# Stick-breaking attention: the second sigmoid and the running product moved from PSUM to SBUF, and the PSUM banks dealt out anew

## The chip, the cores and the metric

The kernel runs on one core of a Trainium2 chip. A core has a matrix engine (PE, with its weight loader PEld), a vector engine (DVE), an activation engine (ACT), a general engine (POOL) and DMA queues issued by SP. Each engine runs its own instructions in their written order and waits on semaphores for the others. Operands live in SBUF; matmuls write to PSUM, which has eight banks of 128 partitions by 512 fp32. POOL does not touch PSUM in this kernel. The metric is device time in microseconds, the median of several executions.

## What is computed

One decoder block in fp32 over 2048 tokens of width 1024: an input projection, eight attention heads beside a pooling branch, an output projection, then a gated feed-forward layer. The change touches the attention alone:

```python
for i in range(S // Q_BLOCK):                      # 128 queries at a time
    L = (i + 1) * Q_BLOCK
    z = jnp.einsum('bhqd,bhkd->bhqk', qb, kb) * inv_sqrt
    mask = s_idx < t_idx
    log1m = jnp.where(mask, -jax.nn.softplus(z), 0.0)
    after = lax.cumsum(log1m, axis=3, reverse=True) - log1m
    logw = jax.nn.log_sigmoid(z) + after
    w = jnp.where(mask, jnp.exp(jnp.where(mask, logw, 0.0)), 0.0)
    outs.append(jnp.einsum('bhqk,bhkd->bhqd', w, vb))
```

The kernel writes this without logarithms: the weight of key s is sigmoid(z_s) times the product of sigmoid(-z_j) over the later keys j up to the query. That product is a scan from right to left along a row.

## The kernel before

Matmuls run in single-pass fp32 with each operand split into a high and a low part (`split`, L57 to L60: ACT writes the high part, DVE or POOL subtracts to get the low one), so one product is two or three matmuls (`mm3`, L65 to L71).

**The attention stage** goes through 80 units (head h, query block tb, key block sc), with sc from tb down to 0, and 4 steps in each unit, one for each 128 queries: 320 steps. A unit with sc == tb is *diagonal*: its step i needs only (i+1)*128 keys, and a mask is added by one more matmul. All others are *full*, 128 queries by 512 keys in each step. In step n the program emits, in this order:

1. `weights_step` (L792): two matmuls make z in a PSUM bank (L801, L802), ACT takes sigmoid(z/8) to `sg` in SBUF (L806), and sigmoid(-z/8) in place in the z bank (L807).
2. `scan_step` (L810) of step n-1: POOL sets the column past the row's end, to 1 in a diagonal unit (L815) or to the product carried over from the key block to the right (L817); DVE scans the z bank from right to left into `pr` in SBUF (L818), starting from that same carry, which it reads out of the earlier `pr`; POOL multiplies `sg` by the shifted `pr` into `w` (L821). The scan's second tensor operand is not used (its operation is a bypass); `sg` is given for it.
3. `values_step` (L839), three turns behind: two matmuls add to `av`, the sum for (h, tb), over four to sixteen turns (L848, L849). After the last, ACT copies `av` to `o1` in SBUF (L853) and two DMAs store it.
4. `turn_step` (L825), seven steps behind the weights: PE transposes the `w` tiles into a PSUM bank (L833), ACT writes the high part `wth` (L59), DVE the low part `wtl` (L60).
5. Now and then a filler piece: three matmuls of the input projection for tokens still to come, in a bank of its own, with the work that goes with it.

No planner reorders this: every engine gets its instructions in the order in which the program emits them. The banks are dealt in turn: three for z, two for turned weights (`wt`), two for `av`, one for fillers (`mm`). A bank comes free when the last reader of what stood in it is done, and the next matmul into it waits for that. In SBUF there are five `sg` tiles, six `pr`, eleven `w` (OFF + 4), and four each of `wth` and `wtl`.

Of the kernel before, what the change touches and what calls it, by code (L numbers as in the profile page):

```python
# [9 lines left out]
F32 = mybir.dt.float32  # L10
F32R = mybir.dt.float32r
AF = mybir.ActivationFunctionType
ALU = mybir.AluOpType
# [4 lines left out]
P = 128  # L18
# [10 lines left out]
TB = 512  # L29
# [3 lines left out]
NEG = -1e30  # L33
LAG = 2
OFF = 7
ZB, WB = 3, 2
FT = {"sr": 4, "p1": 1, "u2": 2, "u3": 2, "u4": 1, "cu": 2, "s": 6, "gs": 3, "tr": 4, "gf": 1}
PAIRS, HELD = 6, 4
RB = PAIRS - 1
# [5 lines left out]
def block_kernel(ctx, tc, x, c, w_cond, b_cond, g_mix_pre, g_mix_post, w_in, w_pool,  # L45
                 pool_scale, w_out, g_ffn_pre, g_ffn_post, w_gate, w_up, w_down, out):
    nc = tc.nc
# [17 lines left out]
    def mm3(ps, terms, first=True, last=True):  # L65

        n = len(terms)
        for i, ((lh, ll), (rh, rl)) in enumerate(terms):
            nc.tensor.matmul(ps, lh, rh, start=first and i == 0, stop=False)  # L69
            nc.tensor.matmul(ps, lh, rl, start=False, stop=False)  # L70
            nc.tensor.matmul(ps, ll, rh, start=False, stop=last and i == n - 1)  # L71

    def open_pool(stack, name, bufs=1, side=None):
        kw = {"side": side} if side else {}
        return stack.enter_context(tc.tile_pool(name=name, bufs=bufs, reuse_waits="tile", **kw))
# [68 lines left out]
    def psum(tag, bufs, name):  # L144
        return psp.tile([P, TB], F32, tag=tag, bufs=bufs, name=name)

    turn = [0]

    def mm_ps(name, alone=False):
        turn[0] += 1  # L150
        return z_ps(name) if turn[0] % 2 and not alone else psum("mm", 1, name)

    z_ps = lambda name: psum("z", ZB, name)
    t_ps = lambda name: psum("wt", WB, name)
    av_ps = lambda name: psum("av", 2, name)

    ident_r = c1.tile([P, P], F32R, tag="ident_r", name="ident_r")
    nc.vector.tensor_copy(ident_r, ident)
# [2 lines left out]
    one = ones[:, 0:1]  # L161
# [149 lines left out]
    def tokens(tb, k, cols=slice(0, TB)):  # L311
        if tb == 1:
            both = ht[1][k // HK]
            return both[:, 0, k % HK, cols], both[:, 1, k % HK, cols]
        return ht[tb][0][:, k, cols], ht[tb][1][:, k, cols]
# [145 lines left out]
    def take_chunk(chunk, tb, ps):  # L461
        kind, m = chunk
        if kind == "u":
            ops = pool_ops(tb, ps, m)
            urgent.append(next(ops))
            small.append(ops)
        else:
            urgent.append(lambda: store_qk(tb, ps, (qd if kind == "q" else kd)[m], f"{kind}{m}"))
# [132 lines left out]
        modulate(1, kc, pt)  # L601

    first_ps = {}
    first_banks = {(0, 0): ("mm", 1), (0, 1): ("av", 2), (1, 1): ("av", 2)}

    def first_products(n, tb, *ks):
        if (n, tb) not in first_ps:
            first_ps[n, tb] = psum(*first_banks.get((n, tb), ("z", ZB)), f"first{n}_{tb}")
        ps = first_ps[n, tb]
        for k in ks:  # L610
            mm3(ps, [((loaded[n][1][:, k, :], loaded[n][2][:, k, :]), tokens(tb, k))], first=k == 0, last=k == KC - 1)
        if ks[-1] == KC - 1:
            take_chunk(chunks[n], tb, ps)
# [156 lines left out]
    att = open_pool(ph1, "att", bufs=2)  # L770
# [14 lines left out]
        nc.sync.dma_start(raw(vt), vd[tb][:, h, :].rearrange("(b p) e -> p b e", p=P))  # L785
        return qt

    qts, prevs, avs, wss = {}, {}, {}, {}

    scans = []  # L790

    def weights_step(u, i):  # L792

        h, tb, sc = u
        diag = sc == tb
        kt, qt = kv[h, sc][0], qts[h, tb]
        L = (i + 1) * P if diag else TB
        nm = f"{h}_{tb}_{sc}_{i}"
        z = z_ps(f"z{nm}")
        keys = kt[:, 0:L]  # L800
        nc.tensor.matmul(z[:, 0:L], qt[:, 0, i * P:(i + 1) * P], keys, start=True, stop=False)  # L801
        nc.tensor.matmul(z[:, 0:L], qt[:, 1, i * P:(i + 1) * P], keys, start=False, stop=not diag)  # L802
        if diag:
            nc.tensor.matmul(z[:, i * P:L], ident_r, neg_r, start=False, stop=True)  # L804
        sg = att.tile([P, TB], F32, tag="sg", bufs=5, name=f"sg{nm}")
        nc.scalar.activation(sg[:, 0:L], z[:, 0:L], AF.Sigmoid, scale=0.125)  # L806
        nc.scalar.activation(z[:, 0:L], z[:, 0:L], AF.Sigmoid, scale=-0.125)  # L807
        scans.append((u, i, z, sg, L, nm))

    def scan_step(u, i, z, sg, L, nm):  # L810

        diag = u[1] == u[2]
        pr = att.tile([P, TB + 1], F32, tag="pr", bufs=6, name=f"pr{nm}")
        if diag:
            nc.gpsimd.memset(pr[:, L:L + 1], 1.0)  # L815
        else:
            nc.gpsimd.tensor_copy(pr[:, L:L + 1], prevs[i][:, 0:1])  # L817
        nc.vector.tensor_tensor_scan(pr[:, 0:L][:, ::-1], z[:, 0:L][:, ::-1], sg[:, 0:L],  # L818
                                     one if diag else prevs[i][:, 0:1], ALU.mult, ALU.bypass)
        w = att.tile([P, TB], F32, tag="w", bufs=OFF + 4, name=f"w{nm}")  # L820
        nc.gpsimd.tensor_tensor(w[:, 0:L], sg[:, 0:L], pr[:, 1:L + 1], ALU.mult)  # L821
        prevs[i] = pr
        wss.setdefault(u, []).append(w)

    def turn_step(u, b):  # L825

        h, tb, sc = u
        i0 = b if sc == tb else 0
        lo0 = i0 * P
        nm = f"{h}_{tb}_{sc}_{b}"  # L830
        wt = t_ps(f"wt{nm}")
        for i in range(i0, 4):
            nc.tensor.transpose(wt[:, i * P:(i + 1) * P], wss[u][i][:, b * P:(b + 1) * P], ident)  # L833
        wh = att.tile([P, TB], F32R, tag="wth", bufs=4, name=f"wth{nm}")
        wl = att.tile([P, TB], F32R, tag="wtl", bufs=4, name=f"wtl{nm}")
        split(wh[:, lo0:], wl[:, lo0:], wt[:, lo0:])
        return wh, wl, lo0

    def values_step(u, b, wh, wl, lo0):  # L839
        h, tb, sc = u  # L840
        hp, j = h // 2, h % 2
        first = sc == tb and b == 0
        last = sc == 0 and b == 3
        if first:
            avs[h, tb] = av_ps(f"av{h}_{tb}")
        av = avs[h, tb]
        vb = kv[h, sc][1][:, b, :]
        nc.tensor.matmul(av[:, lo0:], vb, wh[:, lo0:], start=first, stop=False)  # L848
        nc.tensor.matmul(av[:, lo0:], vb, wl[:, lo0:], start=False, stop=last)  # L849
        if last:  # L850
            end = (h, tb) == (HEADS - 1, NTB - 1)
            o1 = (up if end else wsp).tile([P, TB], F32, tag="um" if end else "o1", bufs=1, name=f"o1_{h}_{tb}")
            nc.scalar.copy(o1, av)  # L853
            for part, dst in enumerate((mtd, mld)):
                (nc.scalar if end else nc.sync).dma_start(dst[tb][hp, j * DH:(j + 1) * DH, :], o1[part * DH:(part + 1) * DH])

    def unit_loads(u):
        h, tb, sc = u
        if sc == tb:
            qts[h, tb] = block_loads(h, tb)  # L860
# [23 lines left out]
        next(fill)  # L884
    taken = START
    attending = True
    steps = [(u, i) for u in units for i in range(4)]

    def wo_load():
# [5 lines left out]

    SEQUENCE = [sb * NT // 2 + half * 4 + i for sb in range(2) for i in range(4) for half in range(2)]
    mixed = {}
    banks = itertools.cycle([("z", ZB)] * ZB + [("mm", 1)] + [("wt", WB)] * WB + [("av", 2)] * 2)
    f_ps = lambda name: psum(*next(banks), name)

    def mix_load(T):
        tb, cols = T // 4, slice((T % 4) * P, (T % 4 + 1) * P)
# [48 lines left out]
    waiting = []  # L951
    spent = 0.0
    for n in range(len(steps) + OFF):
        if n < len(steps):
            u, i = steps[n]
            if i == 0:
                unit_loads(u)
            weights_step(u, i)
            spent += 2.5 if u[1] == u[2] else 4.0
        if len(scans) > 1 or n >= len(steps) and scans:  # L960
            scan_step(*scans.pop(0))
        if len(waiting) > LAG:
            values_step(*waiting.pop(0))
        if n >= OFF:
            u, b = steps[n - OFF]
            waiting.append((u, b, *turn_step(u, b)))
        goal = START + (N_PIECES - START) * spent / (4 * sum(area[:END]))
        while fill is not None and taken < goal:
            taken += 1
            if next(fill, 0) == 0:  # L970
                fill = None
        for pool, here in ((hb, not wo and taken >= HB_FREE), (ha, len(wo) == 4 and fill is None)):
            if here:
                hi, lo = (pool.tile([P, 4, D], F32R, tag=tag, name=f"wo_{pool.name}{tag}")
                          for tag in ("hi", "lo"))
# [596 lines left out]
```

## Time and profile before

| | |
|---|---|
| median of 3 runs | 2353.89 us (2349.65 to 2355.68) |
| the profiled execution | 2351.43 us |
| its span, first to last instruction | 2349.6 us |
| mean granted PE clock | 0.991 of full speed |
| attention stage | from 323.5 us (first z) to about 864 us |

The page gives each engine's busy time, then the span in 40 slices of 58.7 us with the busy share of each in tenths, then the groups of instructions. In a group's row stand line, engine, operation, result and operands with their shapes, the count, the busy time and the mean duration in ns of one, and behind the second bar the idle time of the engine just before these instructions and what ended it. A wait for several semaphores is put down to the one that came last by the profile; where the engine named had long been done, it was another. Matmuls are pipelined, so their recorded durations overlap. In a timeline row stand start and duration in us, and in brackets the idle time before it.

### The profile page before, as it was taken

What the parts mean: (1) busy time and instruction counts of PE and PEld (TensorE: products, weight loads), DVE (VectorE), ACT (ScalarE), POOL (GpSimd) and SP (SyncE); (2) the same over time, 40 slices, a digit from 0 to 9 for tenths busy, and PEclk for the clock granted to TensorE, in tenths of its full rate; (3) what the DMA queues carried; (4) which work ended last, traced back from release to release, by engine and by line L of the source; (5) the groups of instructions that cost most, each with busy time, mean ns of one, the idle gap of its engine ahead of it and who ended that gap; (6) DMA issues with size and microseconds to landing.
All of it is one profiled execution on the core that took longest, in us unless ns stands there. A gap on an engine that the chain in (4) does not pass through costs nothing.

```text
span 2349.6 us, 33532 instructions
## 1 busy us (share of the span) xinstructions
PE 2278.4 (97%) x10717; PEld 1866.6 (79%) x10717; DVE 1638.0 (70%) x2221; ACT 1179.3 (50%) x2411; POOL 1293.3 (55%) x1429
## 2 busy tenths in 40 slices
PE   6999999999999989999999999999999999999997
PEld 3778878888888768887888888788888888888885
DVE  6764549999999975757565565886776565555556
ACT  4323659899998864444222232454533323234444
POOL 4542337787677764544777778430475665641004
PEclk9999999999999999999999999999999999999998
DMA  8785764333443636656554555776763333327554
GB/s 287 244 293 193 273 189 117 90 105 90 126 113 95 190 99 196 220 193 203 163 167 153 162 161 179 264 243 201 257 196 101 119 110 95 114 86 279 193 196 144
DMA packets 307116, 405.18 MB, mean 172 GB/s; under 512 B 19254, under 2 KB 179578, under 8 KB 303868
## 3 DMA queue, kind: packets, MB, share of 16 engines
q1 hardware_dynamic: 302620, 400.68, 52.8%
q10 hardware_dynamic: 4320, 2.36, 0.4%
q8 instruction: 85, 1.39, 0.2%
q14 instruction: 91, 0.75, 0.1%
HBM read 274.51 MB, written 128.45 MB: 171 GB/s over the span
## 4 chain that ended last, share of the span: by engine, by line
PE 79%; DVE 7%; issue 4%; ACT 4%; POOL 3%; DMA 3%; SPq 0%; DVEq 0%; POOLq 0%; ACTq 0%
PE t_u L70 3%; PE t_u L69 3%; PE t_u L71 3%; PE t_g L70 3%; PE t_g L69 3%; PE t_g L71 3%; PE wt L833 3%; PE dn0p L70 3%; PE dn0p L71 3%; PE dn0p L69 3%; PE dn1p L70 3%; PE dn1p L69 3%; PE dn1p L71 3%; DVE pr L818 3%; PE b_g L70 2%
## 5 line engine op out<-in xcount | busy, mean ns | idle before, releaser
L821 POOL TENSOR_TENSOR w<-sg,pr 128x512 f32<-128x512 f32 (+2 forms) x320 | 306.1, 956 | 143.6 <-DVE pr L818 81.3
L1179 POOL TENSOR_TENSOR s<-s,cu 128x512 f32<-128x512 f32 x88 | 132.7, 1515 | 240.7 <-DVE cu L1178 140.1
L818 DVE TENSOR_TENSOR_SCAN pr<-z,pr,sg 128x512 f32<-128x512 f32 x192 | 244.5, 1274 | 0.5 <-POOL pr L817 0.5
L60 DVE TENSOR_TENSOR wtl<-wt,wth 128x512 fp32r<-128x512 f32 (+1 forms) x320 | 190.3, 595 | 35.0 <-ACT wth L59 33.0
L806 ACT ACTIVATE sg<-z 128x512 f32<-128x512 f32 (+2 forms) x320 | 175.0, 547 | 48.0 <-PE z L804 22.2
L59 ACT CAST wth<-wt 128x512 fp32r<-128x512 f32 (+1 forms) x320 | 173.1, 541 | 21.5 <-PE wt L833 19.8
L833 PE MATMUL wt<-ident,w 128*128 128x128 f32 x1088 | 172.0, 273 | 2.5 <-DVE wtl L60 2.2
L807 ACT ACTIVATE z<-z 128x512 f32<-128x512 f32 (+2 forms) x320 | 174.1, 544 | 0.0
L60 DVE TENSOR_TENSOR u_s_l<-u_s,u_s_h 128x512 fp32r<-128x512 f32 x66 | 66.4, 1007 | 151.9 <-ACT u_s_h L59 151.9
L833 PEld LDWEIGHTS wt<-ident,w 128*128 128x128 f32 x1088 | 133.5, 140 | 32.6 <-DVE wtl L60 3.7
L1169 ACT ACTIVATE s<-s 128x512 f32<-128x512 f32 x88 | 55.7, 633 | 192.6 <-DVE s L1168 192.6
L801 PE MATMUL z<-kt,qt 128*128 128x512 f32 (+2 forms) x320 | 128.8, 403 | 16.8 <-DVE pr L818 12.2
L70 PE MATMUL dn0p<-w0p_l,g0p_h 128*128 128x512 f32 x308 | 121.2, 394 | 1.9 <-DVE w0p_l L60 1.9
L848 PE MATMUL av<-wth,vt 128*128 128x512 f32 (+1 forms) x320 | 121.5, 380 | 0.0
L60 DVE TENSOR_TENSOR u_a_l<-u,u_a_h 128x512 fp32r<-128x512 f32 x66 | 77.4, 1175 | 62.3 <-ACT u_a_h L59 62.3
L69 PE MATMUL dn0p<-w0p_h,g0p_h 128*128 128x512 f32 x308 | 120.5, 391 | 0.0
L71 PE MATMUL dn0p<-w0p_h,g0p_l 128*128 128x512 f32 x308 | 120.4, 391 | 0.0
L59 ACT CAST g_s_h<-g_s 128x512 fp32r<-128x512 f32 x66 | 39.5, 620 | 157.6 <-POOL g_s L1111 81.5
L849 PE MATMUL av<-wtl,vt 128*128 128x512 f32 (+1 forms) x320 | 116.9, 365 | 0.0
L802 PE MATMUL z<-kt,qt 128*128 128x512 f32 (+2 forms) x320 | 116.7, 365 | 0.0
L59 ACT CAST u_s_h<-u_s 128x512 fp32r<-128x512 f32 x66 | 38.6, 614 | 152.2 <-POOL u_s L1111 152.2
L70 PE MATMUL dn1p<-w1p_l,g1p_h 128*128 128x512 f32 x292 | 114.4, 392 | 0.0
(655 smaller groups left out, 7266.2 us busy)
## 6 DMA issues: line engine op xcount, KB each, us to landing
g<-in_w_gate_dram SPq DMA_DIRECT2D x42, 512.0 KB, 4.6
u<-in_w_up_dram SPq DMA_DIRECT2D x42, 512.0 KB, 5.0
wc<-in_w_cond_dram SPq DMA_DIRECT2D x32, 512.0 KB, 5.8
qt<-qd SPq DMA_DIRECT2D x64, 256.0 KB, 3.9
wd<-in_w_down_dram SPq DMA_DIRECT2D x44, 256.0 KB, 3.0
tdt<-wd SPq DMA_DIRECT2D x44, 256.0 KB, 2.0
w0p<-tdt SPq DMA_DIRECT2D x44, 256.0 KB, 2.9
w1p<-tdt SPq DMA_DIRECT2D x44, 256.0 KB, 2.8
```

Of the source, the lines that this page charges most:

```text
L59: nc.scalar.copy(hi, src)
L60: low.tensor_tensor(lo, src, raw(hi), ALU.subtract)
L69: nc.tensor.matmul(ps, lh, rh, start=first and i == 0, stop=False)
L70: nc.tensor.matmul(ps, lh, rl, start=False, stop=False)
L71: nc.tensor.matmul(ps, ll, rh, start=False, stop=last and i == n - 1)
L801: nc.tensor.matmul(z[:, 0:L], qt[:, 0, i * P:(i + 1) * P], keys, start=True, stop=False)
L806: nc.scalar.activation(sg[:, 0:L], z[:, 0:L], AF.Sigmoid, scale=0.125)
L807: nc.scalar.activation(z[:, 0:L], z[:, 0:L], AF.Sigmoid, scale=-0.125)
L818: nc.vector.tensor_tensor_scan(pr[:, 0:L][:, ::-1], z[:, 0:L][:, ::-1], sg[:, 0:L], one if diag else prevs[i][:, 0:1], ALU.mult, ALU.bypass)
L821: nc.gpsimd.tensor_tensor(w[:, 0:L], sg[:, 0:L], pr[:, 1:L + 1], ALU.mult)
L833: nc.tensor.transpose(wt[:, i * P:(i + 1) * P], wss[u][i][:, b * P:(b + 1) * P], ident)
L1179: nc.gpsimd.tensor_tensor(s, s, u, ALU.mult)
```

## The change

The second sigmoid goes from the z bank to the `pr` tile in SBUF, so `pr` is now taken in `weights_step`; the scan runs in place in `pr`. For its unused operand it gets `idle`, a PSUM bank filled with zeros once. The carry is copied by POOL to a small tile of its own (`carry`, one column) after each scan that has a key block to its left: 192 of the 320. `values_step` moves from behind the scan to the head of the step. The banks are dealt anew during the attention: two for z, one for `idle`, three for turned weights, one for `av`, one for fillers. `bank_cycle` hands out single banks in turn; before and after the attention it gives the same turns as before.

```diff
-        nc.scalar.activation(z[:, 0:L], z[:, 0:L], AF.Sigmoid, scale=-0.125)
-        scans.append((u, i, z, sg, L, nm))
+        pr = att.tile([P, TB + 1], F32, tag="pr", bufs=PRB, name=f"pr{nm}")
+        nc.scalar.activation(pr[:, 0:L], z[:, 0:L], AF.Sigmoid, scale=-0.125)
+        scans.append((u, i, pr, sg, L, nm))
...
-        pr = att.tile([P, TB + 1], F32, tag="pr", bufs=6, name=f"pr{nm}")
-        if diag:
+        carry = carries.pop(i, None)
+        if carry is None:
             nc.gpsimd.memset(pr[:, L:L + 1], 1.0)
         else:
-            nc.gpsimd.tensor_copy(pr[:, L:L + 1], prevs[i][:, 0:1])
-        nc.vector.tensor_tensor_scan(pr[:, 0:L][:, ::-1], z[:, 0:L][:, ::-1], sg[:, 0:L],
-                                     one if diag else prevs[i][:, 0:1], ALU.mult, ALU.bypass)
+            nc.gpsimd.tensor_copy(pr[:, L:L + 1], carry)
+        nc.vector.tensor_tensor_scan(pr[:, 0:L][:, ::-1], pr[:, 0:L][:, ::-1], idle[:, 0:L],
+                                     one if carry is None else carry, ALU.mult, ALU.bypass)
+        if u[2]:
+            carries[i] = att.tile([P, 1], F32, tag=f"carry{i}", bufs=2, name=f"carry{nm}")
+            nc.gpsimd.tensor_copy(carries[i], pr[:, 0:1])
...
+    idle = psum("z2", 1, "idle")
+    nc.vector.memset(idle, 0.0)
+    z_ps, t_ps, av_ps, mm_only = bank_cycle(*('z0', 'z1')), bank_cycle(*('w0', 'w1', 'a1')), bank_cycle(*('a0',)), bank_cycle(*('mm',))
...
     for n in range(len(steps) + OFF):
+        if len(waiting) > LAG:
+            values_step(*waiting.pop(0))
         if n < len(steps):
...
             scan_step(*scans.pop(0))
-        if len(waiting) > LAG:
-            values_step(*waiting.pop(0))
```

What this does to the order on PE is seen at the unit (head 4, query block 2, key block 0). In a name such as `z4_2_0_1` stand head, query block, key block and step; the last number is the buffer's. PE before, from one z to the next, with the engines whose semaphores a row waits for:

```order
L801 MATMUL z4_2_0_0_7300<-kt4_0_6774,qt4_2_7096 128x512 [waits DVE_49,Activation_49]
L802 MATMUL z4_2_0_0_7300<-kt4_0_6774,qt4_2_7096 128x512
L848 MATMUL av4_1_7164<-wth4_1_0_2_7241,vt4_0_6775 128x512 [waits Activation_49]
L849 MATMUL av4_1_7164<-wtl4_1_0_2_7242,vt4_0_6775 128x512
L833 MATMUL wt4_2_2_1_7313<-ident_180,w4_2_2_1_7162 128x128 [waits DVE_49]
L833 MATMUL wt4_2_2_1_7313<-ident_180,w4_2_2_2_7183 128x128
L833 MATMUL wt4_2_2_1_7313<-ident_180,w4_2_2_3_7210 128x128
L801 MATMUL z4_2_0_1_7321<-kt4_0_6774,qt4_2_7096 128x512 [waits DVE_49,Activation_49]
```

PE with the change, the same step:

```order
L853 MATMUL av4_1_7357<-wth4_1_0_2_7454,vt4_0_6972 128x512 [waits Activation_49]
L854 MATMUL av4_1_7357<-wtl4_1_0_2_7455,vt4_0_6972 128x512
L803 MATMUL z4_2_0_0_7519<-kt4_0_6971,qt4_2_7301 128x512 [waits Activation_49]
L804 MATMUL z4_2_0_0_7519<-kt4_0_6971,qt4_2_7301 128x512
L838 MATMUL wt4_2_2_1_7532<-ident_180,w4_2_2_1_7372 128x128 [waits PE_49]
L838 MATMUL wt4_2_2_1_7532<-ident_180,w4_2_2_2_7394 128x128
L838 MATMUL wt4_2_2_1_7532<-ident_180,w4_2_2_3_7423 128x128
L853 MATMUL av4_1_7357<-wth4_1_0_3_7485,vt4_0_6972 128x512 [waits Activation_49]
L854 MATMUL av4_1_7357<-wtl4_1_0_3_7486,vt4_0_6972 128x512 [waits DVE_49]
L803 MATMUL z4_2_0_1_7546<-kt4_0_6971,qt4_2_7301 128x512 [waits Activation_49]
```

The values pair now stands ahead of z, and z waits for ACT alone; the wait for DVE has gone to the pair's second matmul, which reads `wtl`, and the transposes stand right behind z.

On ACT, at the end of query block 1 in the same unit, before the change:

```order
L806 ACTIVATE sg4_2_0_1_7324<-z4_2_0_1_7321 128x512 [waits PE_49,Pool_49]
L807 ACTIVATE z4_2_0_1_7321<-z4_2_0_1_7321 128x512 [waits DVE_49,Activation_49]
L853 COPY o1_4_1_7334<-av4_1_7164 128x512 [waits DMAHW2_49,DMAHW1_49,PE_49]
L59 CAST wth4_2_2_2_7341<-wt4_2_2_2_7338 128x256 [waits PE_49]
L806 ACTIVATE sg4_2_0_2_7351<-z4_2_0_2_7348 128x512 [waits PE_49,Pool_49]
```

and with it:

```order
L59 CAST wth4_2_2_1_7536<-wt4_2_2_1_7532 128x384 [waits DVE_49,PE_49]
L858 COPY o1_4_1_7542<-av4_1_7357 128x512 [waits DMAHW2_49,DMAHW1_49,PE_49]
L808 ACTIVATE sg4_2_0_1_7549<-z4_2_0_1_7546 128x512 [waits PE_49,Pool_49]
L810 ACTIVATE pr4_2_0_1_7551<-z4_2_0_1_7546 128x512
L59 CAST wth4_2_2_2_7560<-wt4_2_2_2_7557 128x256 [waits DVE_49,PE_49]
```

The copy of the finished sum, `o1`, has moved ahead of the step's two sigmoids.

More of the change, by code (lines that the diff above doesn't have):

```diff
@@ L35 @@
 OFF = 7
-ZB, WB = 3, 2
+PRB = 6
 FT = {"sr": 4, "p1": 1, "u2": 2, "u3": 2, "u4": 1, "cu": 2, "s": 6, "gs": 3, "tr": 4, "gf": 1}
@@ L150, in mm_ps, with bank_cycle @@
         turn[0] += 1
[L151 to L155, printed above, removed]
+        return z_ps(name) if turn[0] % 2 and not alone else mm_only(name)
+    def bank_cycle(*tags):
+        tags = itertools.cycle(tags)
+        return lambda name: psum(next(tags), 1, name)
+    z_ps, t_ps, av_ps, mm_only = bank_cycle("z0", "z1", "z2"), bank_cycle("w0", "w1"), bank_cycle("a0", "a1"), bank_cycle("mm")
     ident_r = c1.tile([P, P], F32R, tag="ident_r", name="ident_r")
@@ L603, in block_kernel @@
     first_ps = {}
-    first_banks = {(0, 0): ("mm", 1), (0, 1): ("av", 2), (1, 1): ("av", 2)}
+    first_banks = {(0, 0): mm_only, (0, 1): av_ps, (1, 1): av_ps}
     def first_products(n, tb, *ks):
         if (n, tb) not in first_ps:
-            first_ps[n, tb] = psum(*first_banks.get((n, tb), ("z", ZB)), f"first{n}_{tb}")
+            first_ps[n, tb] = first_banks.get((n, tb), z_ps)(f"first{n}_{tb}")
         ps = first_ps[n, tb]
@@ L786, in block_loads @@
         return qt
-    qts, prevs, avs, wss = {}, {}, {}, {}
+    qts, carries, avs, wss = {}, {}, {}, {}
     scans = []
@@ L806, in weights_step, with scan_step @@
         nc.scalar.activation(sg[:, 0:L], z[:, 0:L], AF.Sigmoid, scale=0.125)
-        nc.scalar.activation(z[:, 0:L], z[:, 0:L], AF.Sigmoid, scale=-0.125)
-        scans.append((u, i, z, sg, L, nm))
-    def scan_step(u, i, z, sg, L, nm):
+        pr = att.tile([P, TB + 1], F32, tag="pr", bufs=PRB, name=f"pr{nm}")
+        nc.scalar.activation(pr[:, 0:L], z[:, 0:L], AF.Sigmoid, scale=-0.125)
+        scans.append((u, i, pr, sg, L, nm))
+    def scan_step(u, i, pr, sg, L, nm):
         diag = u[1] == u[2]
-        pr = att.tile([P, TB + 1], F32, tag="pr", bufs=6, name=f"pr{nm}")
-        if diag:
+        carry = carries.pop(i, None)
+        if carry is None:
             nc.gpsimd.memset(pr[:, L:L + 1], 1.0)
         else:
-            nc.gpsimd.tensor_copy(pr[:, L:L + 1], prevs[i][:, 0:1])
-        nc.vector.tensor_tensor_scan(pr[:, 0:L][:, ::-1], z[:, 0:L][:, ::-1], sg[:, 0:L],
-                                     one if diag else prevs[i][:, 0:1], ALU.mult, ALU.bypass)
+            nc.gpsimd.tensor_copy(pr[:, L:L + 1], carry)
[4 more added lines that the diff above has]
+            nc.gpsimd.tensor_copy(carries[i], pr[:, 0:1])
         w = att.tile([P, TB], F32, tag="w", bufs=OFF + 4, name=f"w{nm}")
         nc.gpsimd.tensor_tensor(w[:, 0:L], sg[:, 0:L], pr[:, 1:L + 1], ALU.mult)
-        prevs[i] = pr
         wss.setdefault(u, []).append(w)
@@ L897, in block_kernel @@
     mixed = {}
-    banks = itertools.cycle([("z", ZB)] * ZB + [("mm", 1)] + [("wt", WB)] * WB + [("av", 2)] * 2)
-    f_ps = lambda name: psum(*next(banks), name)
+    f_ps = bank_cycle("z0", "z1", "z2", "mm", "w0", "w1", "a0", "a1")
     def mix_load(T):
```

## The prediction

> **What bounds the kernel now.** I read the page's head and slices first, then the busy time by stage, then the attention stage alone, by line and engine.
>
> ```profile
> span 2349.6 us, 33532 instructions
> PE 2278.4 (97%) x10717; PEld 1866.6 (79%) x10717; DVE 1638.0 (70%) x2221; ACT 1179.3 (50%) x2411; POOL 1293.3 (55%) x1429
> PE   6999999999999989999999999999999999999997
> DVE  6764549999999975757565565886776565555556
> ```
>
> The attention stage is slices 6 to 14 of the DVE row. There PE and DVE both read 9, elsewhere only PE does. Two rows by stage, one from inside it and all that follows it, say how full (columns: stretch, length, then busy time and count of PE, PEld, DVE, ACT, POOL, the granted clock, DMA).
>
> ```profile
> 600.00:700.00 100.00, 98.32 (x564) 81.82 (x563) 95.93 (x126) 90.58 (x201) 68.94 (x130) 1.00 0.41 114
> 900.00:2350.00 1450.00, 1426.63 (x6293) 1171.71 (x6291) 928.25 (x1261) 553.68 (x1056) 762.00 (x550) 1.00 0.54 175
> ```
>
> After 900 us DVE is 64% busy and the diff touches nothing there, so the whole difference must arise between 323 and 864 us, and a saving there passes through to the end. In that stage PE's 98% overstates it: matmuls overlap (in the timeline below a pair recorded as 0.39 us each takes 620.66 to 621.13, so 0.23 us each). DVE's 96% hardly does. These are its groups in 323 to 864 us, with the idle time before each:
>
> ```profile
> L818 DVE TENSOR_TENSOR_SCAN pr<-z,pr,sg 128x512 f32<-128x512 f32 x192 | 244.5, 1274 | 0.5 <-POOL pr L817 0.5
> L60 DVE TENSOR_TENSOR wtl<-wt,wth 128x512 fp32r<-128x512 f32 (+2 forms) x315 | 186.8, 593 | 27.1 <-ACT wth L59 25.1
> L818 DVE TENSOR_TENSOR_SCAN pr<-z,ones,sg 128x128 f32<-128x128 f32 (+3 forms) x128 | 111.4, 873 | 1.3 <-POOL pr L815 0.8 <-ACT z L807 0.5
> L60 DVE TENSOR_TENSOR k<-k,k 128x512 fp32r<-128x512 f32 x7 | 4.8, 682 | 4.4 <-ACT k L59 4.4
> ```
>
> DVE's idle time is 0.5 + 27.1 + 1.3 + 4.4 = 33.3 us. The 4.4 is one wait for a chunk of k and the change does not reach it, so 28.9 us is the ceiling of what better feeding of DVE can give. Nearly all of it is DVE waiting for the turned weights (wtl behind ACT's wth, behind PE's transposes). PE in turn waits here:
>
> ```profile
> L801 PE MATMUL z<-kt,qt 128*128 128x512 f32 (+2 forms) x320 | 128.8, 403 | 16.8 <-DVE pr L818 12.2 <-ACT sg L806 1.4 <-ACT o L853 0.8
> L801 PEld LDWEIGHTS z<-kt,qt 128*128 128x128 f32 x320 | 60.1, 188 | 42.6 <-ACT sg L806 14.6 <-ACT z L807 8.4 <-ACT wth L59 4.6
> ```
>
> Ahead of z the matmul side idles 16.8 us and the weight side 42.6 us; the true stall lies between. The names after the arrows mislead: ACT's share of a z bank is long done when the scan of it still runs. One full step of head 4 shows it:
>
> ```profile
> 618.70 1.27 DVE L818 TENSOR_TENSOR_SCAN pr<-z,pr,sg 128x512 f32<-128x512 f32 x1
> ...
> 619.89 0.67 DVE L60 TENSOR_TENSOR wtl<-wt,wth 128x512 fp32r<-128x512 f32 x1
> ...
> 620.12 0.47 PE L801 MATMUL z<-kt,qt 128*128 128x512 f32 x1
> ...
> 620.48 1.27 DVE L818 TENSOR_TENSOR_SCAN pr<-z,pr,sg 128x512 f32<-128x512 f32 x1
> 620.66 0.39 PE L848 MATMUL av<-wth,vt 128*128 128x512 f32 x1
> ...
> 621.13 0.49 PE L833 MATMUL wt<-ident,w 128*128 128x128 f32 x3
> ...
> 621.90 0.47 PE L801 MATMUL z<-kt,qt 128*128 128x512 f32 x1 [0.27 <-DVE pr L818]
> ...
> 622.67 0.39 PE L849 MATMUL av<-wtl,vt 128*128 128x512 f32 x1
> ...
> 623.70 0.59 ACT L853 COPY o<-av 128x512 f32<-128x512 f32 x1
> ```
>
> Both z start 0.15 us after a scan ends (618.70 + 1.27 = 619.97, z at 620.12; 620.48 + 1.27 = 621.75, z at 621.90). Three z banks, each held until its scan is over, chain PE to DVE: in full units DVE is the bound and PE stands. In diagonal units it turns round, since their scans are short. Units of head 4:
>
> ```profile
> 591.82:597.31 5.49, 5.49 (x36) 4.64 (x35) 5.49 (x9) 4.82 (x12) 2.56 (x9) 1.00 0.89 267
> 597.31:603.89 6.58, 6.58 (x39) 5.49 (x38) 5.69 (x10) 5.75 (x13) 3.72 (x10) 1.00 0.21 59
> 610.42:616.33 5.91, 5.91 (x38) 5.21 (x38) 5.14 (x9) 5.29 (x13) 4.41 (x10) 1.00 0.24 52
> 616.33:630.32 13.99, 13.34 (x75) 10.71 (x74) 13.99 (x19) 12.63 (x28) 9.54 (x17) 1.00 0.59 167
> 630.32:636.89 6.57, 6.57 (x40) 5.50 (x39) 5.70 (x10) 5.16 (x12) 3.15 (x9) 1.00 0.30 84
> ```
>
> The four diagonal units (all rows but the fourth) leave DVE idle 0, 0.89, 0.77 and 0.87 us, 0.63 on the mean, while PE is busy throughout; the two full units of the fourth row leave it idle 0. Times 32 diagonal units that is 20 of the 28.9 us. So PE has too small a lead when it enters a diagonal unit, and the lead is capped by the z banks.
>
> **The change part by part.** First, z leaves its bank after ACT's second sigmoid, and z(n) then waits for the sigmoids of step n-2 instead of the scan of step n-3. Second, the values products move ahead of z in a step and turned weights get a third bank. PE's limit becomes: the values pair needs the wtl of three steps back, which ends as the scan of step n-3 starts (619.89 + 0.67 against 620.48 in the rows). That is 1.2 us earlier than z could go before; z follows the values pair 0.47 us later (620.66 to 621.13), so it may run 0.7 us earlier, and the transposes, which no longer stand behind the values pair, 1.2 us earlier. ACT takes them in the order sg, pr, wth, so what reaches DVE is the smaller, 0.7 us. A lead 0.7 us larger covers the mean loss of 0.63 us, not a loss of 0.89, and not two diagonal units with one full unit between. I count three quarters of 28.9 us: 21.5. The ends: 0 if nothing is covered, 28.9 if all is.
>
> Prices on the other engines:
>
> ```profile
> L806 ACT ACTIVATE sg<-z 128x512 f32<-128x512 f32 x224 | 137.0, 611 | 30.4 <-PE z L802 18.6 <-PE z L804 6.6 <-POOL pr L815 1.4
> L807 ACT ACTIVATE z<-z 128x512 f32<-128x512 f32 x224 | 136.3, 609 | 0.0
> L853 ACT COPY o<-av 128x512 f32<-128x512 f32 x31 | 18.6, 600 | 0.3 <-DMA mld<-o 0.3
> L817 POOL COPY pr<-pr 128x1 f32<-128x1 f32 x192 | 35.9, 187 | 0.0
> ```
>
> ACT: the first sigmoid already goes from PSUM to SBUF and takes 611 ns, the second inside PSUM 609; 320 times 2 ns is 0.6 us, on an engine that is 90% busy: 0. [...]
>
> POOL: 192 carry copies of 187 ns are 36 us more, on an engine 69% busy in the row of 600 to 700 us. They stand between the scan and w, so w ends 0.2 us later; its transposes come at least three steps of 1.78 us (619.97 to 621.75) after the scan. The scan waits for a carry made four steps before. Cost 0, with w's lateness as the part that could cost if POOL falls behind. DVE gets one fill of the idle bank, at most 0.7 us.
>
> The single values bank is the new wait. At a change of (head, query block) the next values pair waits for o, and z is now queued behind that pair. In the timeline the last values matmul ends at 622.67 + 0.39 = 623.06 and o starts 0.64 us later, at 623.70, behind the step's two sigmoids; the change puts it ahead of them. PE has z and transposes, about 1.0 us (620.12 to 621.13), between the two pairs and, with a filler piece of three matmuls, 0.7 us more; o's start (0.64), its length (0.6) and the release (0.15) are 1.4 at most. So 0 with a filler, up to 0.5 without: 31 times 0.5 is 15.5 at the most, 0 at the least. I take 3, since fillers stand in most steps.
>
> The scan itself: one operand in PSUM, one in SBUF, result in SBUF, as now; 1274 ns stays. The rows that say how it could move are the shortest scan (by shape) and two operations told by tile, each with its shortest, median and longest duration in ns:
>
> ```profile
> L818 DVE TENSOR_TENSOR_SCAN pr<-z,ones,sg 128x128 f32<-128x128 f32 x32 | 15.1, 473 | 0.0
> ```
>
> ```profile
> L60 DVE TENSOR_TENSOR u_s_l<-u_s,u_s_h x66: 674/1124/1767, 1076.4 to 2105.5; 128x512 fp32r<-128x512 f32 x66
> L1178 DVE TENSOR_TENSOR cu<-t_u,u3u x44: 673/682/694, 1106.0 to 2116.2; 128x512 f32<-128x512 f32 x44
> ```
>
> Two SBUF operands (u_s_l) stretch to 1767 ns beside a busy POOL, one from PSUM (cu) never above 694; the idle bank keeps the scan in the second kind.
>
> Sum against the profiled execution's 2351.4 us (span 2349.6): minus 21.5, plus 3, plus 0.6 is about minus 18, 2333.4. The median of the runs, 2353.9, stands 2.5 above that execution, so 2336.
>
> **The rivals.**
>
> *No change.* PE, not its lead, is the limit in diagonal units, and the stall removed at z returns at the values pair and the transposes. For it: PE is busy 6.58 of 6.58 us. Against: between 16.8 and 42.6 us of waiting before z, which PE could have spent on the diagonal units' work. Time about 2352, a little of the lead being of use.
>
> *Slower, by the single values bank.* If ACT is late by its two sigmoids (1.2 us) whenever o comes up, a handover costs PE up to 1.7 us. At 0.9 us each, 31 of them eat the 21.5 and 7 more; from there it decides. At 1.2 us: 37 minus 21.5, 2369. Against: o is now ahead of those sigmoids, and a handover in a stretch where DVE is the bound costs nothing.
>
> *Slower, by sharing.* The in-place scan reads and writes one SBUF tile while POOL works; if it stretched like u_s_l's median (1124 against 674, 0.45 us), 224 full scans cost 101 us: about 2437. The wtl rows (same mix of operands) speak against it. [...]
>
> [...]
>
> **How the numbers follow.** My forecast has 0.70 (its own range 2326 to 2346), no change 0.14, the values bank 0.07, sharing 0.03, the shorter scan 0.06. Within 0.3% (7 us) a measurement of this kernel cannot tell a change. Faster is 0.70 + 0.06 = 0.76, same 0.14, slower 0.10. The range reaches down to 2318, where DVE's idle time is all gone with a little of the shorter scan, and up to 2354, no change; both slower cases stay out.
>
> **What would show it.** Right: no z waiting for a scan; wtl's idle time down from 27.1 to under 10 us; scans still 1274 ns; the stage shorter by 15 to 22 us, all else equal. The values bank would show as PE idle before the values pair until ACT's o ends; sharing as scans above 1274 ns; no change as idle time before the values pair or the transposes in place of that before z. The forecast is wrong if ACT's queue, 90% busy, is what keeps wth late: then DVE's wait stays though z never waits.

## The result and the profile after

| kernel | median | ratio to before, 95% interval |
|---|---|---|
| before | 2351.77 us (2349.41 to 2355.68) | |
| changed | 2335.65 us (2332.90 to 2339.16) | 0.9931 [0.9910, 0.9952] |
| changed, timed again (before beside it: 2352.60) | 2337.88 us (2333.55 to 2340.95) | 0.9937 [0.9924, 0.9949] |

The change gains 15 to 16 us, 0.6 to 0.7%. The page of the changed kernel has these lines for the span, the busy time of the engines, and the slices of PE and DVE:

```profile
span 2334.4 us, 33386 instructions
PE 2268.4 (97%) x10717; PEld 1863.7 (80%) x10717; DVE 1633.2 (70%) x2222; ACT 1165.1 (50%) x2411; POOL 1317.9 (56%) x1621
PE   6999999999999999999999999999999999999997
DVE  6774559999999966756666665886766555565556
```

The one slice in which PE had read 8 is gone. To see the stage alone, take it from the start of its first scan to the end of its last one (length, then busy time and count of PE, PEld, DVE, ACT, POOL, the granted clock, DMA). Before:

```profile
325.97:861.52 535.55, 516.68 (x2936) 427.34 (x2937) 507.44 (x649) 477.85 (x1051) 394.12 (x715) 1.00 0.41 119
```

and after:

```profile
324.31:846.82 522.51, 509.85 (x2949) 427.97 (x2950) 501.92 (x649) 464.08 (x1052) 417.90 (x907) 1.00 0.43 122
```

The stage is 13.0 us shorter. The span is 15.2 us shorter; the other 2.2 us are an earlier start of the stage (1.7) and 0.5 behind it, where the program does the same work. In the rows of other kernels below, the stage starts anywhere from 324.39 to 326.07, so these 2.2 us are no more than scatter.

Length minus busy time is what an engine stood idle. PE stood 18.9 us before and 12.7 after, DVE 28.1 and 20.6. Where PE stands now is read from the groups of the changed kernel in 323 to 850 us, with the idle time behind the second bar:

```profile
L821 DVE TENSOR_TENSOR_SCAN pr<-pr,carry,idle 128x512 f32<-128x512 f32 x192 | 244.3, 1272 | 0.0
L60 DVE TENSOR_TENSOR wtl<-wt,wth 128x512 fp32r<-128x512 f32 (+2 forms) x316 | 187.2, 593 | 21.1 <-ACT wth L59 19.8
L808 ACT ACTIVATE sg<-z 128x512 f32<-128x512 f32 (+2 forms) x319 | 180.5, 566 | 53.6 <-PE z L806 23.2 <-PE z L804 17.8 <-POOL w L827 3.4
L810 ACT ACTIVATE pr<-z 128x512 f32<-128x512 f32 (+2 forms) x319 | 179.6, 563 | 0.0
L838 PE MATMUL wt<-ident,w 128*128 128x128 f32 x1072 | 171.3, 274 | 3.7 <-POOL w L827 1.9 <-POOL pr L818 1.8
L853 PE MATMUL av<-wth,vt 128*128 128x512 f32 (+2 forms) x314 | 126.9, 404 | 5.9 <-ACT o L858 5.8
L803 PE MATMUL z<-kt,qt 128*128 128x512 f32 (+2 forms) x319 | 117.7, 369 | 1.9 <-ACT pr L810 1.3 <-DMA vt<-vd 0.4
L854 PE MATMUL av<-wtl,vt 128*128 128x512 f32 (+2 forms) x313 | 116.1, 371 | 1.7 <-DVE wtl L60 1.3
L803 PEld LDWEIGHTS z<-kt,qt 128*128 128x128 f32 x318 | 60.0, 189 | 12.8 <-ACT pr L810 3.3 <-ACT wu_h L59 0.8
L853 PEld LDWEIGHTS av<-wth,vt 128*128 128x128 f32 x314 | 59.5, 190 | 20.5 <-ACT o L858 12.5
```

No wait of z for DVE is left; the matmul side of z stands 1.9 us where it stood 16.8. For the other PE lines before, which the prediction did not show:

```profile
L833 PE MATMUL wt<-ident,w 128*128 128x128 f32 x1068 | 169.0, 273 | 2.5 <-DVE wtl L60 2.2
L848 PE MATMUL av<-wth,vt 128*128 128x512 f32 (+2 forms) x312 | 118.3, 379 | 0.0
L849 PE MATMUL av<-wtl,vt 128*128 128x512 f32 (+2 forms) x312 | 113.7, 365 | 0.0
```

So on PE the account of the 13.0 us is: 14.9 less before z, 5.9 and 1.7 more before the two values matmuls, 1.2 more before the transposes (together 6.1 less idle), and 6.8 us less recorded busy time. What the transposes wait for has changed too: before, 2.2 of their 2.5 us were DVE's `wtl`, now all 3.7 us, in five waits, are put down to POOL. The new wait for the single values bank depends on what PE has to do in between. Here is a change of query block late in the stage with no filler piece in its step (PE and ACT; start and duration in us, idle time in brackets):

```profile
830.33 0.38 PE L838 MATMUL wt<-ident,w 128*128 128x128 f32 x2
830.51 0.60 ACT L59 CAST wth<-wt 128x384 fp32r<-128x384 f32 x1
830.87 0.73 ACT L858 COPY o<-av 128x512 f32<-128x512 f32 x1
831.65 0.50 PE L853 MATMUL av<-wth,vt 128*128 128x512 f32 x1 [0.95 <-ACT o L858]
```

and one in head 4 with a filler piece, the three matmuls of L69 to L71:

```profile
612.96 0.38 PE L838 MATMUL wt<-ident,w 128*128 128x128 f32 x2
613.10 0.48 PE L69 MATMUL q<-hth,wq_h 128*128 128x512 f32 x1
613.30 0.62 ACT L858 COPY o<-av 128x512 f32<-128x512 f32 x1
613.41 0.40 PE L70 MATMUL q<-htl,wq_h 128*128 128x512 f32 x1
613.64 0.40 PE L71 MATMUL q<-hth,wq_l 128*128 128x512 f32 x1
613.97 0.50 PE L853 MATMUL av<-wth,vt 128*128 128x512 f32 x1
```

Both times the values pair starts 0.05 us after `o` ends (831.60 and 613.92). In the first, PE's transposes end at 830.71 and PE stands 0.95 us; in the second the filler fills the wait, and the pair starts 0.33 us after the last filler matmul, where 0.23 would have done. The waits of the changed kernel in this stage count it (total us, times, longest):

```profile
PEld av L853 <- ACT o L858: 12.5, 23, 1.2
```

The weight side waited for `o` 23 times, at 31 changes of query block or head. The matmul side is split by the fillers: counted over the trace, 18 of the 31 changes have a filler between transposes and values pair, and PE stands 0.07 us in all there; the 13 without stand 5.8 us, 0.45 each.

### The profile page after: what moved, and what is told of

Read it like the earlier page. It is cut to its first block, busy times and chain, and to the rows that moved or that the text cites. A ratio compares the mean times of both kernels' runs of the same rounds, so it can differ in the third digit from the quotient of the medians.

```text
span 2334.4 us, 33386 instructions
## 1 busy us (share of the span) xinstructions
PE 2268.4 (97%) x10717; PEld 1863.7 (80%) x10717; DVE 1633.2 (70%) x2222; ACT 1165.1 (50%) x2411; POOL 1317.9 (56%) x1621
## 4 chain that ended last, share of the span: by engine, by line
PE 81%; DVE 5%; POOL 4%; DMA 4%; issue 3%; ACT 2%; SPq 1%; POOLq 0%; DVEq 0%; ACTq 0%
PE wt L838 4%; PE t_u L71 3%; PE t_u L70 3%; PE t_u L69 3%; PE t_g L70 3%; PE t_g L69 3%; PE t_g L71 3%; PE dn0p L70 3%; PE dn0p L71 3%; PE dn0p L69 3%; PE dn1p L69 3%; PE dn1p L70 3%; PE dn1p L71 3%; PE av L853 3%; PE av L854 2%
## 5 line engine op out<-in xcount | busy, mean ns | idle before, releaser
L821 DVE TENSOR_TENSOR_SCAN pr<-pr,carry,idle 128x512 f32<-128x512 f32 x192 | 244.3, 1272 | 0.0
L808 ACT ACTIVATE sg<-z 128x512 f32<-128x512 f32 (+2 forms) x320 | 180.8, 565 | 56.2 <-PE z L806 25.8
L59 ACT CAST wth<-wt 128x512 fp32r<-128x512 f32 (+1 forms) x320 | 179.5, 562 | 12.8 <-PE wt L838 12.8
L810 ACT ACTIVATE pr<-z 128x512 f32<-128x512 f32 (+2 forms) x320 | 179.9, 562 | 0.0
L853 PE MATMUL av<-wth,vt 128*128 128x512 f32 (+1 forms) x320 | 129.2, 404 | 5.9 <-ACT o L858 5.8
L69 PE MATMUL dn0p<-w0p_h,g0p_h 128*128 128x512 f32 x308 | 120.5, 391 | 0.0
L71 PE MATMUL dn0p<-w0p_h,g0p_l 128*128 128x512 f32 x308 | 120.4, 391 | 0.0
L803 PE MATMUL z<-kt,qt 128*128 128x512 f32 (+2 forms) x320 | 117.9, 369 | 1.9 <-ACT pr L810 1.3
L804 PE MATMUL z<-kt,qt 128*128 128x512 f32 (+2 forms) x320 | 117.0, 366 | 0.0
```

Source lines behind the costliest of these rows:

```text
L59: nc.scalar.copy(hi, src)
L810: nc.scalar.activation(pr[:, 0:L], z[:, 0:L], AF.Sigmoid, scale=-0.125)
L821: nc.vector.tensor_tensor_scan(pr[:, 0:L][:, ::-1], pr[:, 0:L][:, ::-1], idle[:, 0:L], one if carry is None else carry, ALU.mult, ALU.bypass)
```

## The experiments

The questions, in the order in which they arose: which part of the change brings the gain; what the single values bank costs; what the idle PSUM operand is for; and which engine bounds the stage now. Each edit is against the changed kernel unless it says otherwise. All ratios are to the kernel before, timed beside (2352.74, 2353.03 and 2352.60 us).

**Everything but the scan's move.** The second sigmoid stays in PSUM, the scan reads z; third bank for turned weights, single values bank and the new order stay, with three z banks; POOL's carry copies fall away, as the scan does not overwrite the earlier `pr`.

```diff
-        nc.scalar.activation(pr[:, 0:L], z[:, 0:L], AF.Sigmoid, scale=-0.125)
+        nc.scalar.activation(z[:, 0:L], z[:, 0:L], AF.Sigmoid, scale=-0.125)
...
-        nc.vector.tensor_tensor_scan(pr[:, 0:L][:, ::-1], pr[:, 0:L][:, ::-1], idle[:, 0:L],
+        nc.vector.tensor_tensor_scan(pr[:, 0:L][:, ::-1], z[:, 0:L][:, ::-1], sg[:, 0:L],
...
-    idle = psum("z2", 1, "idle")
-    nc.vector.memset(idle, 0.0)
-    z_ps, ... = bank_cycle(*('z0', 'z1')), ...
+    z_ps, ... = bank_cycle(*('z0', 'z1', 'z2')), ...
```

> Everything but the move to SBUF: second sigmoid in place in PSUM, scan from there, banks z three, turned weights three, sums one, fillers one, values step first. Theory A (z's bank held by the scan is what caps PE's lead): z still waits for the scan of step n-3 and now stands behind the values pair, so 2350 to 2358 us. If the third bank and the order carried the gain by themselves: 2336 to 2343 us.

Measured: 2353.00 us, ratio 1.0000 [0.9991, 1.0009]. Nothing is left of the gain in the time. Its groups in 323 to 862 us show why:

```profile
L803 PE MATMUL z<-kt,qt 128*128 128x512 f32 (+2 forms) x320 | 122.5, 383 | 10.5 <-DVE pr L821 9.0
```

z still waits for the scan, and the values bank's wait is added to it. Without the scan's move the rest is worth nothing that the time shows. In the profiled execution its stage takes 532.07 us, 3.5 less than before, but what follows the stage takes 3.2 us more (1491.2 against 1488.1); a few us of one execution lie within such scatter.

**The scan's move alone.** The old order, two banks for turned weights, two for values:

```diff
-... bank_cycle(*('z0', 'z1')), bank_cycle(*('w0', 'w1', 'a1')), bank_cycle(*('a0',)), ...
+... bank_cycle(*('z0', 'z1')), bank_cycle(*('w0', 'w1')), bank_cycle(*('a0', 'a1')), ...
...
-        if len(waiting) > LAG:
-            values_step(*waiting.pop(0))
         if n < len(steps):
...
             scan_step(*scans.pop(0))
+        if len(waiting) > LAG:
+            values_step(*waiting.pop(0))
```

> Only the move of the second sigmoid and the scan to SBUF: step order as before, banks z two, idle one, turned weights two, sums two, fillers one. Theory A (PE's lead): z waits for ACT only, but the transposes stand behind the values pair and wait for the low part of two steps back, so about half the gain, 2342 to 2346 us. Theory C (bank of turned weights or step order carries the gain): 2350 to 2354 us. If the z banks were all: 2333 to 2338 us.

Measured: 2340.60 us, 0.9948 [0.9935, 0.9960]. Some three quarters of the gain (12.1 us against 14.7 to 16.1), more than the half that was expected. The stall has moved on to the transposes; its waits in 323 to 850 us:

```profile
PEld wt L838 <- DVE wtl L60: 20.4, 37, 2.2
PE wt L838 <- DVE wtl L60: 8.7, 27, 1.8
```

With two banks for turned weights, the transposes need the `wtl` of two turns back. That is the wait which the third bank takes away.

**Order and banks apart.** With the scan moved, the old order on the new banks, and the new order on the old two and two:

```diff
 # old order, new banks
-        if len(waiting) > LAG:
-            values_step(*waiting.pop(0))
         if n < len(steps):
...
             scan_step(*scans.pop(0))
+        if len(waiting) > LAG:
+            values_step(*waiting.pop(0))
 # new order, two and two banks
-... bank_cycle(*('w0', 'w1', 'a1')), bank_cycle(*('a0',)), ...
+... bank_cycle(*('w0', 'w1')), bank_cycle(*('a0', 'a1')), ...
```

> The changed kernel with the values step back behind z, banks as changed (z two, idle, turned weights three, sums one, fillers one). With two banks for turned weights the old step order was the faster one (2340.6 against 2345.7 us). Theory A, the order decides through what waits for DVE's low part: with three banks the transposes no longer wait for DVE, so old and new order come out within 4 us of 2335.7. Theory D, the new order is needed for the gain of the third bank (then z and the transposes both stand behind the values pair only once): 2340 us or more.

> The changed kernel with two banks for the values sum and two for turned weights (z two, idle one, fillers one). In the changed kernel the first values pair of a new query block starts 0.05 us after o ends at 22 of 31 changes, and the matmul side and the weight side idle 5.8 and 12.5 us there. Theory A, that wait gives back part of the gain: without it 2326 to 2331 us against 2335.7 of the changed kernel. Theory B, PE waits there only where DVE is the bound, so it costs nothing: 2334 to 2337. Theory C, the third bank for turned weights is what carries the gain: 2340 or more.

Measured: 2343.95 us, 0.9959 [0.9946, 0.9972], and 2345.74 us, 0.9976 [0.9967, 0.9985]. The old order on the new banks waits longer for the finished sum, since `o` stands behind two sigmoids; in its groups of 323 to 857 us:

```profile
L853 PE MATMUL av<-wth,vt 128*128 128x512 f32 (+2 forms) x313 | 121.4, 388 | 9.3 <-ACT o L858 9.1
```

The new order on two and two banks stands before the transposes, in 323 to 853 us:

```profile
L838 PE MATMUL wt<-ident,w 128*128 128x128 f32 x1068 | 173.7, 277 | 14.8 <-DVE wtl L60 11.6 <-POOL pr L818 1.3 <-POOL pr L820 0.3
```

The third bank pays 8 to 10 us in the new order although it takes the second values bank; these intervals part. By the medians each of the two alone is 3 to 5 us worse than neither (2340.60), and both together are 3 to 5 us better; there the intervals overlap, but for the new order alone.

**The first values pair later.** The first values pair of each head and query block, the only one that waits for `o`, goes to the end of its step, behind transposes and fillers:

```diff
     for n in range(len(steps) + OFF):
-        if len(waiting) > LAG:
+        due = len(waiting) > LAG
+        fresh = due and waiting[0][1] == 0 and waiting[0][0][1] == waiting[0][0][2]
+        if due and not fresh:
             values_step(*waiting.pop(0))
...
                 fill = None
+        if fresh:
+            values_step(*waiting.pop(0))
         for pool, here in ...
```

> The changed kernel with its banks as they are, but the first values step of each (head, query block) at the end of its step, behind transposes and fillers, so that ACT's copy o has some 1 to 1.7 us more. Theory A (the values bank's wait costs): idle time before the first values pair falls from 18 us to under 6, time 2326 to 2331 us. Theory B (it is covered by DVE): 2334 to 2337 us, with the wait gone all the same.

Measured: 2330.64 us, 0.9910 [0.9896, 0.9924], 5.0 us below the changed kernel's first median. Then both again, side by side:

> The changed kernel itself, word for word, timed again beside the next one so that the two can be told apart. Theory C (a single values bank costs PE a wait at most handovers, and its price is what moving the pair behind the transposes gave back): 2334 to 2337 us, and 4 to 6 us above the next kernel. Rival (the 5 us between the two was scatter between batches): the two within 2 us of each other.

> The kernel with the first values pair of each (head, query block) at the end of its step, unchanged from the earlier run, beside the changed kernel. Theory C: 2329 to 2332 us, and below the changed kernel by 4 to 6 us with intervals that part. Rival (scatter): within 2 us of the changed kernel.

Measured: 2337.88 us for the changed kernel and 2329.98 us for the late pair, 0.9937 [0.9924, 0.9949] against 0.9902 [0.9887, 0.9917]. The intervals part; the difference is 7.9 us here, 5.0 the first time. The second run's stage, and its values group in 323 to 846 us:

```profile
325.50:842.28 516.78, 507.15 (x2950) 428.20 (x2951) 500.22 (x649) 462.89 (x1052) 416.73 (x907) 1.00 0.43 123
```

```profile
L853 PE MATMUL av<-wth,vt 128*128 128x512 f32 (+2 forms) x314 | 125.0, 398 | 0.4 <-ACT o L858 0.4
```

The wait for `o` fell from 5.9 to 0.4 us: at the end of its step the pair has a filler ahead of it at 27 of the 31 changes, where 18 had one. PE's idle time fell from 12.7 to 9.6 us, and the stage is 5.7 us shorter again. This version beats both kernels: 22.6 us below before.

**Two operands in SBUF.** The scan gets `sg` for its unused operand, as before the change, in place of the idle PSUM bank:

```diff
-        nc.vector.tensor_tensor_scan(pr[:, 0:L][:, ::-1], pr[:, 0:L][:, ::-1], idle[:, 0:L],
+        nc.vector.tensor_tensor_scan(pr[:, 0:L][:, ::-1], pr[:, 0:L][:, ::-1], sg[:, 0:L],
```

> The changed kernel with the scan's unused operand taken from SBUF (sg) in place of the idle PSUM bank; the result is the same. [...]

Measured: 2500.81 us, 1.0628 [1.0614, 1.0643]; 163 to 165 us above the changed kernel. The scan line and POOL's one-column copy of the carry, with shortest, median and longest duration in ns:

```profile
L821 DVE TENSOR_TENSOR_SCAN pr<-pr,carry,sg x192: 1269/1727/2407, 336.4 to 1004.5; 128x512 f32<-128x512 f32 x192
L820 POOL COPY pr<-carry x192: 174/1114/1210, 338.9 to 1009.6; 128x1 f32<-128x1 f32 x192
```

and the same two lines of the changed kernel:

```profile
L821 DVE TENSOR_TENSOR_SCAN pr<-pr,carry,idle x192: 1269/1272/1279, 332.5 to 845.5; 128x512 f32<-128x512 f32 x192
L820 POOL COPY pr<-carry x192: 175/186/198, 333.4 to 847.5; 128x1 f32<-128x1 f32 x192
```

The shortest scan is the same, 1269 ns, and the spread is 10 ns in the one and 1138 ns in the other. A copy of one column takes six times as long, and it ends with a scan: counted over the trace, 131 of the 132 of these copies that take over 600 ns end 0.02 us before a scan ends. From its first scan to its last the stage takes 678.98 us in place of 522.51; DVE's busy time grew by 132 us (501.92 to 634.25) and POOL's by 216 (417.90 to 633.88), and the transposes stand 84 us for POOL where they stood 3.7, in 323 to 1005 us:

```profile
L838 PE MATMUL wt<-ident,w 128*128 128x128 f32 x1064 | 191.4, 287 | 84.2 <-POOL w L827 57.4 <-POOL pr L818 26.6
```

So the place of the operand that the scan does not even use decides whether DVE and POOL block each other. By what mechanism is not shown.

**Fillers moved out of the diagonal units.** The weight of a diagonal step in the pacing of fillers, 1.5 in place of 2.5, which puts more filler pieces into full units; once in the changed kernel and once in the kernel before:

```diff
-    area = [2.5 if tb == sc else 4.0 for _, tb, sc in units]
+    area = [1.5 if tb == sc else 4.0 for _, tb, sc in units]
...
-            spent += 2.5 if u[1] == u[2] else 4.0
+            spent += 1.5 if u[1] == u[2] else 4.0
```

> The changed kernel with fewer filler pieces in diagonal steps (weight 1.5 in place of 2.5 against 4 for a full step; the number of pieces is the same). Theory E, what is left of DVE's idle time (16 of 20.6 us lie in diagonal units) is PE's own work there: 2325 to 2331 us and DVE idle under 15 us. Theory F, it is latency at the handover of the values bank and ACT's queue: 2333 to 2338 us.

> The kernel before, with the same shift of fillers to full steps. Theory E: PE's work in diagonal units is part of DVE's idle time there too, but PE's lead stays capped by the z banks: 2344 to 2350 us against 2352. If the shift alone does as much as the change: 2338 us or less. If PE's lead is all that counts: 2351 to 2354.

Measured: 2343.28 us, 0.9957 [0.9942, 0.9972], and 2359.49 us, 1.0026 [1.0016, 1.0036]: 5 to 8 and 6.5 us worse by the medians, and outside every range that was expected. In the kernel before that is clear of noise; in the changed kernel the intervals overlap. The stage of the changed kernel with it:

```profile
326.07:856.34 530.27, 513.09 (x2950) 430.27 (x2951) 504.40 (x649) 465.43 (x1052) 417.10 (x907) 0.99 0.43 120
```

PE stands 17.2 us in place of 12.7. So the theory that the diagonal units were short of PE for the fillers' sake is not borne out. Part of what was lost lies before z, 5.6 us in place of 1.9, in 323 to 860 us:

```profile
L803 PE MATMUL z<-kt,qt 128*128 128x512 f32 (+2 forms) x320 | 117.8, 368 | 5.6 <-ACT pr L810 2.4 <-DMA kt<-kd 1.9 <-DMA qt<-qd 1.3
```

That the full units have no PE time to spare either would fit, but is not shown. The other way round, on top of the late first pair:

```diff
+    area = [3.25 if tb == sc else 4.0 for _, tb, sc in units]
...
+            spent += 3.25 if u[1] == u[2] else 4.0
```

> Late first pair, and the weight of a diagonal step in the pacing of the fillers 3.25 in place of 2.5, so that diagonal units get a larger share of the filler pieces and full units a smaller one; the number of pieces stays. With the weight at 1.5 the changed kernel had lost 8 us. Theory F (full units have less of PE to spare than diagonal ones, so the fillers belong into the diagonal units): 2322 to 2328, with less idle time of DVE in the full units. Theory G (2.5 is near the best share, any move costs): 2332 to 2340, with DVE's idle time up in the diagonal units.

Measured: 2329.63 us, 0.9899 [0.9886, 0.9913], the same as the late pair at 2.5 (2329.98). Neither theory came out: between 2.5 and 3.25 the share of fillers makes no difference.

**Half the scan.** The scan of a full step runs over 256 of its 512 columns; half of the running product is left out, all else stays:

```diff
+        S = L if u[1] == u[2] else L // 2
-        nc.vector.tensor_tensor_scan(pr[:, 0:L][:, ::-1], pr[:, 0:L][:, ::-1], idle[:, 0:L],
+        nc.vector.tensor_tensor_scan(pr[:, 0:S][:, ::-1], pr[:, 0:S][:, ::-1], idle[:, 0:S],
```

> The changed kernel with the scan of every full step over the first 256 of its 512 columns only (the other half of the running product is left out; everything else as it was). It takes some 0.53 us (worked out from 872 ns for the mean diagonal scan of 320 columns and 1272 ns for 512) off 192 scans, 102 us of DVE. It asks what bounds the stage behind DVE. Theory A (DVE alone bounds the stage, PE and ACT have room): the time falls by most of it, to 2240 to 2270. Theory H (ACT, 503 us busy in the 525 us of the stage, is close behind): the stage stops near 505 to 512 us, 2316 to 2324, and what DVE still waits for in the changed kernel is ACT's queue as much as PE.

Measured: 2332.99 us, 0.9917 [0.9899, 0.9935], only 3 to 5 us below the changed kernel, and outside both ranges that were expected. Its stage, and three groups of it in 323 to 850 us:

```profile
324.39:842.52 518.13, 506.04 (x2944) 426.68 (x2945) 418.03 (x649) 463.76 (x1052) 416.14 (x906) 1.00 0.43 123
```

```profile
L60 DVE TENSOR_TENSOR wtl<-wt,wth 128x512 fp32r<-128x512 f32 (+2 forms) x317 | 191.5, 604 | 102.8 <-ACT wth L59 96.7
L808 ACT ACTIVATE sg<-z 128x512 f32<-128x512 f32 (+2 forms) x319 | 180.5, 566 | 51.8 <-PE z L806 17.9 <-PE z L804 16.1 <-POOL pr L818 7.7
L822 DVE TENSOR_TENSOR_SCAN pr<-pr,carry,idle 128x256 f32<-128x256 f32 x192 | 141.5, 737 | 0.0
```

The scan went from 1272 to 737 ns and DVE's busy time from 502 to 418 us. Nearly all of it turned into waiting: DVE stands 100.1 us in place of 20.6, and the stage is 4.4 us shorter. ACT, which the second theory named as next, stands 54.4 us, and the largest part of what it waits for ahead of `sg` is PE's z. PE stands 12.1 us, as it did (12.7). So in the changed kernel DVE does not bound the stage, though it is 96% busy (501.92 of 522.51). What does is PE, by what is left over and by an estimate: in the changed kernel the median time from one matmul's start to the next is 0.233 us behind one of 512 columns, 0.18 behind 384, 0.12 behind 256 and 0.109 behind 128. At these intervals the matmuls recorded in the stage take 501.8 of its 522.5 us, and 500.7 of 518.1 with half the scan. No run took work off PE, so this is not shown by experiment. How closely DVE follows isn't measured either; in the run with two SBUF operands DVE grew longer, but POOL more so.

## Why the prediction came out as it did

**The mechanism was right.** "Three z banks, each held until its scan is over, chain PE to DVE": with the scan moved, z's wait is 1.9 us for 16.8; with everything else changed and the scan left, z waits 10.5 and the time is that of before. What is left of z's wait is mostly ACT's second sigmoid (1.3 of the 1.9 us), as foreseen.

**The bound was named wrongly.** The step that failed is "PE's 98% overstates it ... DVE's 96% hardly does". The half scan shows that 84 us less of DVE's work is worth 4 us after the change. Whether DVE was the bound before the change was not tried; the z rows show that PE waited for it then. The slip was to take matmuls that overlap as a sign of room: a pair that takes 0.23 us a piece shows that recorded durations overlap, not that the engine has time between them. The gaps of PE in the stage (18.9 us before, 12.7 after) were the account to start from.

**The gain's term was measured on the wrong engine.** "Three quarters of 28.9 us: 21.5" was to be idle time of DVE. Idle time of DVE fell by 7.5 us (28.1 to 20.6), and wtl's part of it from 27.1 to 21.1, not under 10 as the prediction's sign of being right asked; the stage is 13.0 us shorter, not 15 to 22. Another 5.5 us came off DVE's busy time, mostly because its instructions overlap by 0.08 us when none waits (618.70 + 1.27 against 619.89 in the prediction's rows): counted over the trace, 104 of 647 starts had no such overlap before, 64 after; 40 times 0.08 is 3.2 us. Added up, the overlaps rose from 44.9 to 48.9 us, and the recorded durations fell by 1.5. The sum had no term for that. On PE the same gain reads 14.9 us before z and 6.8 of recorded busy time, 21.7 in all. That this is nearly the predicted 21.5 is chance. The 6.8 can't be put down to one row, but the intervals given at the half scan allow an estimate: at those intervals the recorded matmuls take 499.3 of the 535.6 us before and 501.8 of the 522.5 after. The 36.2 and 20.7 us that are left hold 18.9 and 12.7 of idle time, so 9.3 us of stall inside recorded matmuls went, and 13 more matmuls inside the stage's bounds took 2.5 of it back.

**The new waits were put too low.** For the values bank stood 3 us, since "fillers stand in most steps". Its parts held: "0 with a filler, up to 0.5 without" against 0.07 us at 18 changes and 0.45 each at 13 (0.95 at most). The mean of the 13 is near the upper end, and they alone make 5.8 of the 5.9 us; taking the wait away was worth 5.0 and 7.9 us of time. The rest was not in the sum at all: 1.7 us before the second values matmul, which now reads a `wtl` just in time, and 1.2 before the transposes. In all 8.8 in place of 3.6 with the fill of the idle bank, which took 0.49 us in the trace. The part of the rival "no change" that said the stall would return at the values pair and the transposes held for 8.8 of 21.7 us.

**The zeros held, but for POOL's.** ACT: the second sigmoid, now to SBUF, takes 563 ns against 566 for the first over the same shapes. POOL's carry copies added 23.8 us of busy time (394.12 to 417.90) on an engine that still stands 105 us. But the prediction named "w's lateness as the part that could cost if POOL falls behind", and the matmul side of the transposes now waits for POOL five times, 3.7 us, where it never did before; whether the copies are the cause was not tried. The scan stayed at 1272 ns against 1274. No run shows a scan made shorter by the place of its source, to which 0.06 of the chances and a part of the range's lower end, 2318, were given: the 192 scans that start from a carry took 1267 to 1282 ns before and 1269 to 1279 after. So the shorter scan did not come, and sharing did not either; but sharing is real, with one operand's place between it and this kernel, and at 163 to 165 us it is dearer than the 101 that the rival gave it. The rival counted DVE's scans alone; DVE's busy time grew by 132 us and POOL's, which it left out, by 216.

**The sum.** Minus 18 was forecast against the profiled execution, and its span fell by 15.2, of which the stage gave 13.0. The forecast of 2336 lies 0.4 us from the first median and 1.9 from the second; the terms that made it were 21.5 and 3.6 where PE's account has 21.7 and 8.8. Two pieces of luck closed the distance: the 2.2 us ahead of and behind the stage, and the kernel before, which the forecast took at 2353.9 and which came out at 2351.77 and 2352.60.

**Order and banks.** That they pay only together was not said in the prediction, which counted the third bank as a part of the lead. By the medians they cost 3 to 5 us each alone, and together give 3 to 5 on top of the scan's 12.

## What to carry to other kernels

Before counting one engine's idle time as the ceiling of a gain, cut that engine's work in one trial run and see whether the stage follows. Two engines that are 96 and 98% busy look alike. When a bank is taken from one use for another, look for the one instruction that waits for it at each handover and put something behind which it can hide ahead of it in the queue; here that was worth a third to a half as much as the change itself. An operand that an instruction does not use still has a place, and the place can matter more than the rest of the change: 163 to 165 us here, against the change's 15 to 16.

## What the runs showed of the hardware

A scan of 512 columns with two SBUF operands, in a stage where POOL was 93% busy (633.88 of 678.98 us), took 1727 ns at the median and up to 2407; with one operand in PSUM, and POOL 80% busy (417.90 of 522.51), 1272 and never above 1279. The shortest took 1269 in both. The other side pays more: POOL's copy of one column went from 186 to 1114 ns, and 131 of the 132 that took over 600 ns ended with a scan. And a wait on DVE costs more than its gap in these records: the 0.08 us by which an instruction starts before the last one ends (618.70 + 1.27 against 619.89) is lost as well; 104 of 647 starts went without it before, 64 after.
